# The chunked linear recurrence of a hybrid decoder layer under one list scheduler with the delta rule, with other planning weights

## The chip, the cores and the metric

The kernel runs on one core of a Trainium2 chip. The core has a matrix engine (TensorE, PE in the profile; its weight loads are shown as PEld), VectorE (DVE), ScalarE (ACT), GpSimd (POOL) and SyncE (SP), which issues transfers. Each takes its own instructions strictly in the order in which they were written, and waits at the head of its queue until semaphores of the others allow the next one. The metric is the device time of one execution in microseconds; the kernel before takes 1797.59 us, the median of three runs (1796.06 to 1799.65).

## The reference

One decoder layer on 512 tokens of width 1024, all float32: a SwiGLU block, a mixer, a second SwiGLU block, each with an RMS norm ahead and a residual, and a last norm. The mixer projects the normed input once and cuts the columns into two branches:

```python
o_h = hgrn2_chunked(q_h, k_h, hi, log_f)          # 8 heads: S = diag(f) S + k^T v, o = S^T q
o_h = rmsnorm(o_h, hgrn_out_norm) * silu(hg)
...
qkv = silu(causal_short_conv(concat([gq, gk, gv]), conv_w))
o_g = gated_delta_chunked(q_g, k_g, cv, beta, g)  # 16 value heads: S = a (I - beta k k^T) S + beta k v^T
o_g = rmsnorm(o_g, gdn_out_norm) * silu(gz)
...
y = sigmoid(gate_h) * (o_h @ w_branch_hgrn) + sigmoid(gate_g) * (o_g @ w_branch_gdn)
return y @ w_out
```

The first recurrence has a decay for each channel, so its scores inside a chunk are built by halves (blocks of 1, 2, 4 up to 64 positions). The delta rule needs the inverse of a unit lower triangular matrix of each chunk and head.

## The kernel before, in words

Every product with a weight is made in three float32r passes: a weight slab of 128x512 is loaded (`raw`, three buffers), split into a rounded part on ScalarE (`whi`) and the rest on VectorE (`wlo`, five buffers), and `mm3` adds three matmuls for each block of 128. A product of a transposed projection has 24 matmuls of 512 columns, one of an untransposed pair (`wn`, names V, G and z) 96 of 256 columns. The time axis of 512 is cut into four chunks of 128.

The program has four stretches: the first SwiGLU block, the first recurrence, the delta rule, and the merge with the output projection and the second SwiGLU block.

*The first recurrence.* `ORDER` (L33) is an order written out by hand: Q, F, V and G are projections of a head or a pair of heads, S the scores of two heads (`h_scores`, L513), O a head's output (`h_out`, L563), D the decays of the delta rule (`decays`). What is emitted so is interleaved by the framework's own scheduler, with priorities. In `h_scores` each of seven levels has products `pl` on PE (L538, L548), masked copies on VectorE (L541) or copies on ScalarE (L552), and updates of `qp` (VectorE, L556) and `ke` (GpSimd, L557). `h_out` carries the state over the chunks (L575 to L585) and norms the output with a power on GpSimd (L594).

*The delta rule* is planned by `Desk`, a list scheduler in the kernel. Each piece of work is a generator that asks for an engine and a duration, a buffer, an event or a lag. `Desk.run` steps through a planned time, gives the engine to the ready request of lowest rank, and lets the generator emit its instructions, in an order that the framework then leaves as it is. Only planned durations stand behind that order; the chip runs the queues as they were written. `product` (rank 9, the lowest) takes the dense products in the order in which `loader` chose them from `DENSE`; sixteen gate products (t) are taken when none of the list is allowed. The planned weights:

```python
LAG = 2.8                                     # every transfer
yield "use", "POOL", .62 + .0016 * n * w      # one step of the solve, two instructions
yield "use", "POOL", 1.2; yield "lag", .3     # a power on GpSimd, then its reader on VectorE
```

For each of eight pairs of value heads: `g_e` loads a row of decays to all partitions (gb, L653) and makes exponentials; `g_n` norms the key with a power on GpSimd (L695), whose reader is L700 on VectorE, and makes the score products (pgq, L712) and the matrix (n2, L727); `g_b` sends its diagonal blocks through DRAM (L745, L752), solves them on GpSimd in 31 steps of two instructions (L764, L765), and sends the result back through DRAM (L769 and L776, both on SP); `g_inv` copies it (L800), transposes it (L807) and completes the inverse with products (L821, L831); `g_rec` runs the recurrence over the chunks (L883 to L922), norms with another power (L935) and transposes the output (pto, L952). `keep` writes it to DRAM (od).

The buffers of the first recurrence are reused by the delta rule: `room` claims them, and `more` claims those of the branch outputs once product y7 is done. Both recurrences draw on gb, of which there are two buffers: heads hold qp in it, and `g_e` loads into it.

Of the kernel before, what the change touches and what calls it, by code (L numbers as in the profile page):

```python
# [8 lines left out]
F32 = mybir.dt.float32  # L9
# [23 lines left out]
ORDER = (  # L33
    "Q1 Q0 F5 F0 F1 V0 G0 S0 Q2 O0 Q3 O1 F2 F3 V1 G1 D0 S1 Q4 O2 Q5 O3 F4 V2 G2 S2 Q6 O4 Q7 O5 F6 F7 V3 "
    "G3 S3 O6 O7 "
)
# [7 lines left out]
WB = 5  # L44
# [4 lines left out]
LAG = 2.8  # L49
# [290 lines left out]
def mixer(tc, mp, e):  # L340
# [40 lines left out]
    def natural(i, use):  # L381

        sl = [slab(wn[i][:, q * 512:(q + 1) * 512]) for q in range(4)]
        for half in range(2):
            pt = psd.tile([P, T], F32, tag="mm", name="pnat")
            for s in range(2):
                part(sl, pt, 2 * half + s)
                with tc.high_priority():
                    use(2 * half + s, pt[:, s * 256:(s + 1) * 256])

    def part(sl, pt, t):
        for k in range(KD):
            hi, lo = sl[k // 2]
            c = slice((k % 2) * 256, (k % 2) * 256 + 256)
            mm3(pt[:, t % 2 * 256:t % 2 * 256 + 256], uh[:, k, t * P:(t + 1) * P], ul[:, k, t * P:(t + 1) * P],
                hi[:, c], lo[:, c], k == 0, k == KD - 1)

    def gate(t, o, g):

        th = places["thg"]("thg", (P, 256))  # L400
        act.activation(th, o, AF.Tanh, scale=rhalf[:, t:t + 1])
        dve.scalar_tensor_tensor(g[:, t], th, 1.0, o, op0=ALU.add, op1=ALU.mult)

    def normed(src, out):
        pt = dense(src, KD, ux)
        with tc.high_priority():
            dve.tensor_tensor(out, pt, rbc, op=ALU.mult)

# [27 lines left out]
    def decays():  # L436
        pab = dense(wab, KD, ux, m=64)
        dt_b, a_log = dta[:, 0:1], dta[:, 1:2]
        ab = h[:64, 0]
        pool.memset(ab, 0.0)  # L440
        z = h[:64, 1]
        dve.tensor_tensor(z, pab[:64], rbc[:64], op=ALU.mult)
        z2 = h[:16, 2]
        dve.tensor_scalar(z2, z[:16], dt_b, None, op0=ALU.add)
        w = [h[:16, 3 + i] for i in range(4)]

        dve.scalar_tensor_tensor(w[0], z2, -1.0, z2, op0=ALU.mult, op1=ALU.min)
        act.activation(w[0], w[0], AF.Exp)
        dve.tensor_scalar(w[1], w[0], 1.0, None, op0=ALU.add)
        act.activation(w[2], w[1], AF.Ln)  # L450
        dve.scalar_tensor_tensor(w[3], w[1], 1.0, w[0], op0=ALU.subtract, op1=ALU.subtract)
        dve.tensor_tensor(w[2], w[2], w[3], op=ALU.subtract)
        dve.scalar_tensor_tensor(w[2], z2, 0.0, w[2], op0=ALU.max, op1=ALU.add)
        ea = tm("ea", (16, 1))
        act.activation(ea, a_log, AF.Exp)
        dve.tensor_scalar(ab[:16], w[2], ea, -1.0, op0=ALU.mult, op1=ALU.mult)
        act.activation(ab[32:48], z[32:48], AF.Tanh, scale=0.5)
        dve.tensor_scalar(ab[32:48], ab[32:48], 1.0, 0.5, op0=ALU.add, op1=ALU.mult)
        pn = ps("pn")
        for c in range(NT):  # L460
            pe.transpose(pn[:, c * 64:(c + 1) * 64], ab[:, c * P:(c + 1) * P], ident[:64, :64])
        act.copy(nat, v3(pn[:, :256], NT))
        pg = ps("pg")
        pe.matmul(pg[:, 0:64], tri, g_nat, start=True, stop=True)
        pe.matmul(pg[:, 64:128], ones, g_nat, start=True, stop=True)
        dve.tensor_copy(gx[:, 0:2], pg[:, :128].rearrange("p (a b c) -> p a b c", a=2, b=NT))
        dve.tensor_tensor(ek, gend, gam, op=ALU.subtract)
        act.activation(eg, gam, AF.Exp)
        act.activation(eend, gend, AF.Exp)
        act.activation(ek, ek, AF.Exp)  # L470
# [3 lines left out]
        gt = h[:16, 7]  # L474
        dve.tensor_copy(gt, pgt[:16])
        sp.dma_start(gtd, gt)

    def together(*gens):
        gens = list(gens)
        while gens:  # L480
            gens = [g for g in gens if next(g, gens) is not gens]


    def h_q(hd_):
        qs = ta("qs")
        normed(wt[hd_], qs)
        th = ta("th")
        act.activation(th, qs, AF.Tanh, scale=0.5)
        qq = places[("fs", "ut")[hd_ % 2]]("qq", (P, NT, 192))
        dve.scalar_tensor_tensor(qq[:, :, :P], v3(th, NT), 1.0, v3(qs, NT), op0=ALU.add, op1=ALU.mult)  # L490
        return qq

    def h_f(hd_):
        fs = ta("fs")
        normed(wt[8 + hd_], fs)
        act.activation(fs, fs, AF.Tanh, scale=0.5)
        f = places["at"]("f")
        dve.tensor_scalar(f, fs, cf[:, 1, hd_:hd_ + 1], cf[:, 0, hd_:hd_ + 1], op0=ALU.mult, op1=ALU.add)
        ke = places[("kn", "vb")[hd_ % 2]]("ke")
        dve.tensor_scalar(ke, fs, cf[:, 2, hd_:hd_ + 1], cf[:, 1, hd_:hd_ + 1], op0=ALU.mult, op1=ALU.add)  # L500
        return f, ke

    def h_v(p_):
        v = places["n2"]("v", (P, NT, 256))
        natural(p_, lambda t, o: act.activation(v[:, t], o, AF.Copy, scale=rcol[:, t:t + 1]))
        return v

    def h_g(p_):
        g = places["gz"]("hg", (P, NT, 256))
        natural(4 + p_, lambda t, o: gate(t, o, g))  # L510
        return g

    def h_scores(hd_, qq, f, ke, res):  # L513
        qp = places["gb"]("qp")
        dve.tensor_tensor(v3(qp, NT), qq[:, :, :P], v3(f, NT), op=ALU.mult)
        q4 = qp.rearrange("p (c g b) -> p c g b", c=NT, b=2)
        dve.tensor_copy(qq[:, :, P:192], q4[:, :, :, 1])
        at = places["on"]("ah", (P, NT, P))
        fl = f
        ln_ = "ab"[hd_ % 2]  # L520
# [4 lines left out]
        for i in range(2):  # L525
            dve.tensor_tensor(at[:, 2 * i:2 * i + 2], v3(pd[i][:, :384], 2)[:, :, :P], mid(ident, 2), op=ALU.mult)
        for li, hh in enumerate((1, 2, 4, 8, 16, 32, 64)):
            n2 = T // (2 * hh)
            av = at.rearrange("p c (g two b) -> p c g two b", two=2, b=hh)
            if hh == 1:  # L530
                for i in range(2):
                    dve.copy_predicated(av[:, 2 * i:2 * i + 2, :, 1, 0], mid(hm[:, li].bitcast(I32), 2),
                                        v3(pd[i][:, :384], 2)[:, :, P:192])
            elif hh <= 16:
                pl = ps("pl", ln_)
                qv = qp.rearrange("p (c g two b) -> p c g two b", c=NT, two=2, b=hh)
                for c in range(NT):
                    pe.matmul(pl[:, c * 64:(c + 1) * 64], ke[:, c * P:(c + 1) * P], qv[:, c, :, 1],  # L538
                              start=True, stop=True)
                for c in range(NT):  # L540
                    dve.copy_predicated(av[:, c, :, 1], v3(hm[:, li].bitcast(I32), 64 // hh),  # L541
                                        v3(pl[:, c * 64:(c + 1) * 64], 64 // hh))
            else:
                pl = ps("pl", ln_)
                for c in range(NT):
                    for b in range(64 // hh):
                        s0 = 2 * b * hh
                        pe.matmul(pl[s0:s0 + hh, c * hh:(c + 1) * hh], ke[:, c * P + s0:c * P + s0 + hh],  # L548
                                  qp[:, c * P + s0 + hh:c * P + s0 + 2 * hh], start=True, stop=True)
                for b in range(64 // hh):  # L550
                    s0 = 2 * b * hh
                    act.copy(at[s0:s0 + hh, :, s0 + hh:s0 + 2 * hh], v3(pl[s0:s0 + hh, :NT * hh], NT))  # L552
# [4 lines left out]
            pool.tensor_tensor(kv[:, :, 0], kv[:, :, 0], bc(fv[:, :, 1], hh), op=ALU.mult)  # L557
            fn = (places[("x", "we")[hd_ % 2]] if hh == 1 else places[("w", "ft")[hd_ % 2]] if hh == 2 else tm)(f"fl{hh}", (P, n2))
            dve.tensor_tensor(fn, fv[:, :, 0], fv[:, :, 1], op=ALU.mult)
            fl = fn  # L560
            yield
        res += [qp, ke, at, fl]

    def h_out(hd_, qp, ke, at, fe, v, g):
        hs = slice((hd_ % 2) * P, (hd_ % 2) * P + P)
# [3 lines left out]
        kn = places[("gm", "qm")[hd_ % 2]]("hkn", (P, NT - 1, P))  # L569
# [736 lines left out]
```

## Time and profile before

| | |
|---|---|
| median of three runs | 1797.59 us |
| the profiled execution | 1803.54 us, its span 1801.8 us |
| PE busy | 1698.8 us (94%), 9362 matmuls |
| VectorE, ScalarE, GpSimd busy | 953.7, 698.5, 303.7 us |
| mean granted clock of PE | 0.967 |

The page cuts the span into 40 slices of 45 us:

```profile
PE   7999999999999989799798889889999999999997
...
DVE  4544443346586557447576667645454444444333
...
POOL 2000000001121122630532552620000100000001
PEclk9999999999999969899899999899999999999998
```

A digit is the busy share in tenths, and the last line the clock that the throttle granted to PE, in tenths of full speed. Slices 14 to 28 hold the delta rule. Matmuls are pipelined and their ends are modelled, so "busy" on PE says that work was there, not that it ran at its peak; at half clock the same work takes twice as long and counts as busy throughout.

### The profile page before, as it was taken

What the parts mean: (1) busy time and instruction counts of PE and PEld (TensorE: products, weight loads), DVE (VectorE), ACT (ScalarE), POOL (GpSimd) and SP (SyncE); (2) the same over time, 40 slices, a digit from 0 to 9 for tenths busy, and PEclk for the clock granted to TensorE, in tenths of its full rate; (3) what the DMA queues carried; (4) which work ended last, traced back from release to release, by engine and by line L of the source; (5) the groups of instructions that cost most, each with busy time, mean ns of one, the idle gap of its engine ahead of it and who ended that gap; (6) DMA issues with size and microseconds to landing.
All of it is one profiled execution on the core that took longest, in us unless ns stands there. A gap on an engine that the chain in (4) does not pass through costs nothing. (4 is left out here: it accounts for less than half of the span.)

```text
span 1801.8 us, 25958 instructions
## 1 busy us (share of the span) xinstructions
PE 1698.8 (94%) x9362; PEld 1441.1 (80%) x9362; DVE 953.7 (53%) x1992; ACT 698.5 (39%) x1525; POOL 303.7 (17%) x629
## 2 busy tenths in 40 slices
PE   7999999999999989799798889889999999999997
PEld 5888888889989977578686778678788888888887
DVE  4544443346586557447576667645454444444333
ACT  4433333332343325255455455334433433333222
POOL 2000000001121122630532552620000100000001
PEclk9999999999999969899899999899999999999998
DMA  4223333432222114334134233335753333333333
GB/s 150 93 95 100 94 96 114 114 103 71 71 66 71 42 50 134 102 91 115 47 97 117 62 95 96 96 84 169 232 161 109 123 94 100 94 100 92 96 97 112
DMA packets 142561, 182.16 MB, mean 101 GB/s; under 512 B 53072, under 2 KB 59728, under 8 KB 142432
## 3 DMA queue, kind: packets, MB, share of 16 engines
q1 hardware_dynamic: 142432, 180.49, 34.1%
q8 instruction: 74, 1.21, 0.3%
q14 instruction: 55, 0.45, 0.1%
HBM read 163.64 MB, written 16.81 MB: 100 GB/s over the span
## 5 line engine op out<-in xcount | busy, mean ns | idle before, releaser
L176 PE MATMUL pmm<-uh,whi 128*128 128x512 f32 x1288 | 522.8, 406 | 17.0 <-ACT whi L171 6.0
L178 PE MATMUL pmm<-uh,wlo 128*128 128x512 f32 x1288 | 509.8, 396 | 5.3 <-DVE wlo L1120 5.3
L177 PE MATMUL pmm<-ul,whi 128*128 128x512 f32 x1288 | 510.6, 397 | 2.6 <-DVE ul L203 2.4
L171 ACT CAST whi<-raw 128x512 fp32r<-128x512 f32 (+1 forms) x391 | 239.4, 612 | 542.9 <-PE pmm L177 485.0
L172 DVE TENSOR_TENSOR wlo<-raw,whi 128x512 fp32r<-128x512 f32 (+1 forms) x391 | 269.4, 690 | 296.2 <-ACT whi L171 295.6
L176 PEld LDWEIGHTS pmm<-uh,whi 128*128 128x128 f32 x1288 | 246.4, 191 | 68.8 <-ACT whi L171 6.0
L178 PEld LDWEIGHTS pmm<-uh,wlo 128*128 128x128 f32 x1288 | 245.6, 191 | 58.7 <-DVE wlo L1120 5.9
L177 PEld LDWEIGHTS pmm<-ul,whi 128*128 128x128 f32 x1288 | 246.2, 191 | 54.6 <-DVE ul L203 6.4
L176 PE MATMUL pnat<-whi,uh 128*128 128x256 f32 x512 | 153.3, 301 | 0.6 <-DVE ci L627 0.6
L178 PE MATMUL pnat<-whi,ul 128*128 128x256 f32 x512 | 146.1, 286 | 0.0
L177 PE MATMUL pnat<-wlo,uh 128*128 128x256 f32 x512 | 145.8, 285 | 0.0
L176 PE MATMUL pmm<-gh,whi 128*128 128x512 f32 (+1 forms) x374 | 141.0, 377 | 0.0
L178 PE MATMUL pmm<-gh,wlo 128*128 128x512 f32 (+1 forms) x374 | 140.9, 377 | 0.0
L177 PE MATMUL pmm<-gl,whi 128*128 128x512 f32 (+1 forms) x374 | 140.8, 377 | 0.0
L1120 DVE TENSOR_TENSOR wlo<-raw,whi 128x512 fp32r<-128x512 f32 x144 | 99.4, 694 | 76.6 <-ACT whi L1118 75.4
L1118 ACT CAST whi<-raw 128x512 fp32r<-128x512 f32 x144 | 88.8, 619 | 129.1 <-PE pmm L177 77.7
L214 POOL TENSOR_TENSOR acc<-acc,sqt 128x512 f32<-128x512 f32 x24 | 32.8, 1366 | 583.6 <-ACT sqt L212 583.2
L764 POOL TENSOR_TENSOR fm<-gfs,ft 128x60 f32<-128x60 f32 (+24 forms) x248 | 88.6, 357 | 169.7 <-DMA ft<-hmask 138.0
L176 PEld LDWEIGHTS pnat<-whi,uh 128*128 128x128 f32 x512 | 98.6, 193 | 2.1 <-DVE ci L627 0.8
L177 PEld LDWEIGHTS pnat<-wlo,uh 128*128 128x128 f32 x512 | 98.7, 193 | 0.8
L178 PEld LDWEIGHTS pnat<-whi,ul 128*128 128x128 f32 x512 | 98.4, 192 | 0.1
L765 POOL TENSOR_TENSOR ft<-ft,fm 128x60 f32<-128x60 f32 (+24 forms) x248 | 92.6, 373 | 19.4
(345 smaller groups left out, 2228.3 us busy)
## 6 DMA issues: line engine op xcount, KB each, us to landing
raw<-wt SPq DMA_DIRECT2D x128, 256.0 KB
raw<-w1a SPq DMA_DIRECT2D x88, 256.0 KB
raw<-w1b SPq DMA_DIRECT2D x88, 256.0 KB
raw<-wn SPq DMA_DIRECT2D x64, 256.0 KB
raw<-w2b SPq DMA_DIRECT2D x45, 256.0 KB
raw<-w2a SPq DMA_DIRECT2D x40, 256.0 KB
raw<-wbg SPq DMA_DIRECT2D x32, 256.0 KB
gb<-gtd SPq DMA_DIRECT2D x16, 256.0 KB
```

The lines of the kernel that those rows point to most:

```text
L171: act.copy(hi[:, :f], raw[:, :f])
L172: dve.tensor_tensor(lo[:, :f], raw[:, :f], hi[:, :f].bitcast(F32), op=ALU.subtract)
L176: pe.matmul(pt, ah, bh, start=first, stop=False)
L177: pe.matmul(pt, ah, bl, start=False, stop=False)
L178: pe.matmul(pt, al, bh, start=False, stop=last)
L214: pool.tensor_tensor(acc, acc, s, op=ALU.add)
L764: pool.tensor_tensor(tv, bc(m[:, j + 1:, j], w), t[:, j:j + 1, :w].to_broadcast([P, n, w]), op=ALU.mult)
L765: pool.tensor_tensor(t[:, j + 1:, :w], t[:, j + 1:, :w], tv, op=ALU.add)
L1118: act.copy(hi, raw)
L1120: dve.tensor_tensor(lo, raw, hi.bitcast(F32), op=ALU.subtract)
```

## The change

`ORDER`, the functions that emitted the first recurrence by hand and `room` are removed. Its projections go ahead of the list that `Desk` draws on, and each piece becomes a generator with ranks, buffers and planned durations as the delta rule has them. The arithmetic is the same.

```diff
 DENSE = (
+    "F0 Q0 F1 Q1 V0 G0 F2 Q2 F3 Q3 V1 G1 D0 F4 Q4 F5 Q5 V2 G2 F6 Q6 F7 Q7 V3 G3 "
     "k0 q0 k1 q1 y0 y1 y2 y3 v0 v1 y4 y5 y6 y7 z0 k2 q2 v2 v3 z1 ...
-LAG = 2.8
+LAG = dict(raw=3.2, gb=4, nb=5, m=6, nt=4, tq=8, out=4)
+EASE = 2.5
```

The scores and the output of a head are one generator. Its `ke` updates run in a thread of their own:

```diff
+    def h_head(i):
+        yield "on", ("Q", i), ("F", i)
...
+        yield "get", "gb", 1
...
+        def keys(li, kv, fv, hh):
+            yield "use", "POOL", .88
+            pool.tensor_tensor(kv[:, :, 0], kv[:, :, 0], bc(fv[:, :, 1], hh), op=ALU.mult)
+            D.fire(("ke", i, li))
...
+                yield "get", ln_, 1
+                yield T_(.92 if hh <= 16 else .5)
...
+            D.start((2, i), keys(li, kv, fv, hh))
+            yield V(270)
             dve.tensor_tensor(qv[:, :, 1], qv[:, :, 1], bc(fv[:, :, 0], hh), op=ALU.mult)
```

In the delta rule the powers get slack on both sides, a solve step its new weight, and the store of the solve goes from SyncE to GpSimd:

```diff
         dve.tensor_scalar(rk, sm[:, 0, 0:4], 4.0 * EPS, None, op0=ALU.add)
+        yield "lag", EASE
         yield "use", "POOL", 1.2
         pool.tensor_tensor(rk, rk, mhalf[:, :4], op=ALU.pow)
-        yield "lag", .3
+        yield "lag", EASE
...
-            yield "use", "POOL", .62 + .0016 * n * w
+            yield "use", "POOL", .7 + .004 * n * w
...
-        yield "lag", .3
-        yield S
-        sp.dma_start(nt.rearrange("b q i c -> (b q) i c"), t)
-        yield "lag", LAG
+        yield "use", "POOL", .6
+        pool.dma_start(nt.rearrange("b q i c -> (b q) i c"), t)
+        yield "lag", LAG["nt"]
```

The buffers that pass from one recurrence to the other are claimed one by one, as the heads give them back, and a product is chosen when the events that it needs have come:

```diff
+    def claim(name, tag, n, shape, zero=False):
+        G.setdefault(name, [])
+        yield "on", ("free", tag)
+        for j in range(n):
+            yield "get", "w_" if tag == "w" else tag, 1
+            G[name].append(pl(tag, shape))
...
     def choose():
...
+            need = {"Q": [("pd", i - 2)] if i > 1 else [], "F": [("L", i - 4)] if i > 3 else [],
+                    "V": [("pair", i - 2)] if i > 1 else [], "G": [("pair", i - 2)] if i > 1 else [], "D": [],
+                    "y": [("O", 5), ("S", 6), ("S", 7)], ...
+            if all(n in D.at for n in need) and not (k in "qkv" and under >= CONVS):
+                todo.remove(x)
+                return x
         return gates.pop(0) if gates else None
```

`product` now also makes V, G and D, and waits for each branch input (`("O", kt)`) within a y product. The state buffers (s) of both recurrences are counted too. Neither SwiGLU block nor the merge is touched.

More of the change, by code (lines that the diff above doesn't have):

```diff
@@ L379, in mixer @@
     eye4 = e["hmask"][:, 5:9].rearrange("p a (i c) -> p (a i) c", c=8)
[L381 to L407, printed above, removed]
     dve.tensor_scalar(rhalf, rcol, 0.5, None, op0=ALU.mult)
@@ L434, in mixer @@
     gtd = dr.tile([16, T], F32, name="gtd")
-    def decays():
-        pab = dense(wab, KD, ux, m=64)
+    md = dr.tile([KD, P, T], F32, name="md")
+    td = dr.tile([2 * KD, P, T], F32, name="td")
+    od = dr.tile([VH, P, T], F32, name="od")
+    D = Desk(mm=2, a=2, b=2, d=1, e=1, ta=TA, tm=6, thg=1, raw=RB, w=WB, tq=1, n2=2, gz=2, fs=1, ut=1, kn=3, gm=1,
+             qm=2, gb=2, ln=1, at=4, vb=4, t64=2, on=2, ft=1, x=1, we=1, w_=1, s=3)
+    V = lambda n: ("use", "DVE", 0.21 + 0.001 * n)
+    A = lambda n: ("use", "ACT", 0.2 + 0.0009 * n)
@@ L438, in decays, with place @@
+    T_ = lambda n: ("use", "PE", n)
+    S = ("use", "SP", 0.4)
+    taken = {}
+    def place(tag, name, shape, n):
+        taken[tag] = taken.get(tag, 0) + 1
+        if taken[tag] == n:
+            D.fire(("free", tag))
+        return places[tag](name, shape)
+    def decays(pab):
         dt_b, a_log = dta[:, 0:1], dta[:, 1:2]
         ab = h[:64, 0]
+        yield "use", "POOL", .6
         pool.memset(ab, 0.0)
         z = h[:64, 1]
+        yield "on", "rbc"
+        yield *V(512), 1
@@ L474, in decays, with h_q @@
         gt = h[:16, 7]
+        yield V(512)
         dve.tensor_copy(gt, pgt[:16])
+        D.put("d")
+        yield S
         sp.dma_start(gtd, gt)
[L478 to L484, printed above, removed]
+        yield "lag", LAG["out"]
+        D.fire("decays")
+    def h_q(i, pt):
+        yield "get", "ta", 2
+        yield "on", "rbc"
+        yield *V(512), 1
         qs = ta("qs")
-        normed(wt[hd_], qs)
+        dve.tensor_tensor(qs, pt, rbc, op=ALU.mult)
+        D.put("mm")
+        yield A(512)
@@ L487, in h_q, with h_f @@
         th = ta("th")
         act.activation(th, qs, AF.Tanh, scale=0.5)
-        qq = places[("fs", "ut")[hd_ % 2]]("qq", (P, NT, 192))
+        tag = ("fs", "ut")[i % 2]
+        yield "get", tag, 1
+        yield V(512)
+        qq = hq[i] = place(tag, "qq", (P, NT, 192), 4)
         dve.scalar_tensor_tensor(qq[:, :, :P], v3(th, NT), 1.0, v3(qs, NT), op0=ALU.add, op1=ALU.mult)
-        return qq
-    def h_f(hd_):
+        D.put("ta", 2)
+        D.fire(("Q", i))
+    def h_f(i, pt):
+        yield "get", "ta", 1
+        yield "on", "rbc"
+        yield *V(512), 1
@@ L494, in h_f @@
         fs = ta("fs")
-        normed(wt[8 + hd_], fs)
+        dve.tensor_tensor(fs, pt, rbc, op=ALU.mult)
+        D.put("mm")
+        yield A(512)
         act.activation(fs, fs, AF.Tanh, scale=0.5)
[L497 to L514, printed above, removed]
+        yield "get", "at", 1
+        yield V(512)
+        f = place("at", "f", (P, T), 8)
+        dve.tensor_scalar(f, fs, cf[:, 1, i:i + 1], cf[:, 0, i:i + 1], op0=ALU.mult, op1=ALU.add)
@@ new lines, in h_f, with h_v @@
+        tag = ("kn", "vb")[i % 2]
+        yield "get", tag, 1
+        yield V(512)
+        ke = place(tag, "ke", (P, T), 4)
+        dve.tensor_scalar(ke, fs, cf[:, 2, i:i + 1], cf[:, 1, i:i + 1], op0=ALU.mult, op1=ALU.add)
+        hf[i] = f, ke
+        D.put("ta")
+        D.fire(("F", i))
+    def h_v(i, t, o):
+        yield A(300)
+        act.activation(hv_[i][:, t], o, AF.Copy, scale=rcol[:, t:t + 1])
+        if t % 2:
+            D.put("mm")
+        if t == 3:
+            D.fire(("V", i))
@@ L524, in h_scores @@
                       start=True, stop=True)
-        for i in range(2):
-            dve.tensor_tensor(at[:, 2 * i:2 * i + 2], v3(pd[i][:, :384], 2)[:, :, :P], mid(ident, 2), op=ALU.mult)
+        D.put(tag_q)
+        D.fire(("pd", i))
+        yield "get", "on", 1
+        at = place("on", "ah", (P, NT, P), 8)
+        for q in range(2):
+            yield V(256)
+            dve.tensor_tensor(at[:, 2 * q:2 * q + 2], v3(pd[q][:, :384], 2)[:, :, :P], mid(ident, 2), op=ALU.mult)
+        def keys(li, kv, fv, hh):
+            yield "use", "POOL", .88
+            pool.tensor_tensor(kv[:, :, 0], kv[:, :, 0], bc(fv[:, :, 1], hh), op=ALU.mult)
+            D.fire(("ke", i, li))
+        fl, held = f, "at"
         for li, hh in enumerate((1, 2, 4, 8, 16, 32, 64)):
@@ L546, in h_scores @@
                     for b in range(64 // hh):
                         s0 = 2 * b * hh
[L548 to L552, printed above, removed]
+                        yield A(4 * hh)
@@ L568, in h_out @@
             pe.transpose(pk[:, c * P:(c + 1) * P], ke[:, c * P:(c + 1) * P], ident)
-        kn = places[("gm", "qm")[hd_ % 2]]("hkn", (P, NT - 1, P))
+        tag_n = ("gm", "qm")[i % 2]
+        yield "get", tag_n, 1
+        yield A(384)
+        kn = place(tag_n, "hkn", (P, NT - 1, P), 4)
         act.copy(kn, v3(pk[:, :(NT - 1) * P], NT - 1))
+        D.put("d")
+        yield "get", "a", 1
         po = ps("po", "a")
@@ L585, in h_out @@
                     dve.scalar_tensor_tensor(s2, s, fe[:, c:c + 1], pu[:, :P], op0=ALU.mult, op1=ALU.add)
+                    D.put("s")
                 s = s2
-        ss = tm("hss", (P, NT))
-        on = places[("ln", "t64")[hd_ % 2]]("hon", (P, NT, P))
+                D.put("b")
+        D.put("s")
+        D.put(tag_n)
+        D.put(tag_k)
+        D.put("gb")
+        D.put("on")
+        D.put(held)
+        tag_o = ("ln", "t64")[i % 2]
+        yield "get", tag_o, 1
+        yield "get", "tm", 2
+        ss, rho = tm("hss", (P, NT)), tm("hrho", (P, NT))
+        on = place(tag_o, "hon", (P, NT, P), 4)
         for c in range(NT):
+            yield A(300)
             act.activation(on[:, c], po[:, c * P:(c + 1) * P], AF.Square, accum_out=ss[:, c:c + 1])
-        rho = tm("hrho", (P, NT))
+        yield V(4)
         dve.tensor_scalar(rho, ss, 4.0 / P, 4.0 * EPS * 4.0 * P, op0=ALU.mult, op1=ALU.add)
+        yield "lag", EASE
+        yield "use", "POOL", 1.2
         pool.tensor_tensor(rho, rho, mhalf[:, :NT], op=ALU.pow)
+        yield "lag", EASE
+        yield V(4)
         dve.tensor_tensor(rho, rho, rcol, op=ALU.mult)
         for c in range(NT):
+            yield V(150)
             dve.scalar_tensor_tensor(on[:, c], po[:, c * P:(c + 1) * P], rho[:, c:c + 1], g[:, c, hs],
                                      op0=ALU.mult, op1=ALU.mult)
+        D.put("a")
+        D.put("tm", 2)
+        D.fire(("o", i))
+        yield "get", "d", 1
+        yield T_(.46)
         pt = ps("pt")
@@ L602, in h_out, with h_pair @@
         gn = cs[:, C_HN:C_HN + 1]
-        o2 = op[hd_]("oh", (P, 2, T), F32R)
-        oh, ol = o2[:, 0], o2[:, 1]
+        o2 = op[i]("oh", (P, 2, T), F32R)
+        oh, ol = o_h[i] = o2[:, 0], o2[:, 1]
+        yield A(560)
         act.activation(oh, pt, AF.Copy, scale=gn)
+        yield V(560)
         dve.scalar_tensor_tensor(ol, pt, gn, oh.bitcast(F32), op0=ALU.mult, op1=ALU.subtract)
-        return oh, ol
-    md = dr.tile([KD, P, T], F32, name="md")
-    td = dr.tile([2 * KD, P, T], F32, name="td")
-    od = dr.tile([VH, P, T], F32, name="od")
-    D = Desk(mm=2, a=2, b=2, d=1, e=1, ta=TA, thg=1, gb=2, raw=RB, w=WB, on=2, tq=1)
-    V = lambda n: ("use", "DVE", 0.21 + 0.001 * n)
-    A = lambda n: ("use", "ACT", 0.2 + 0.0009 * n)
-    T_ = lambda n: ("use", "PE", n)
-    S = ("use", "SP", 0.4)
+        D.put("d")
+        D.put(tag_o)
+        D.fire(("O", i))
+    def h_pair(p_):
+        yield "on", ("o", 2 * p_), ("o", 2 * p_ + 1)
+        D.put("n2")
+        D.put("gz")
+        D.fire(("pair", p_))
     def conv(k, i, pt, out, n):
@@ L962, in keep @@
         sp.dma_start(to, tile_)
-        yield "lag", LAG
+        yield "lag", LAG["out"]
         D.put(tag)
@@ L1044, in more @@
         G["tp"].append(e_[:, 3].rearrange("p (a b) -> p a b", a=8))
-    def step(k, i):
-        if k in "QFVG":
-            hp[k, i] = {"Q": h_q, "F": h_f, "V": h_v, "G": h_g}[k](i)
-        elif k == "S":
-            hr[2 * i], hr[2 * i + 1] = [], []
-            together(*[h_scores(j, hp["Q", j], *hp["F", j], hr[j]) for j in (2 * i, 2 * i + 1)])
-        elif k == "O":
-            o_h[i] = h_out(i, *hr[i], hp["V", i // 2], hp["G", i // 2])
-        elif k == "D":
-            decays()
-    for w in ORDER.split():
-        step(w[0], int(w[1:]))
+        D.fire("more")
@@ L1112, in maker @@
     def maker(key, raw):
-        yield "lag", LAG
+        yield "lag", LAG["raw"]
         yield "get", "w", 1
@@ L1126, in product @@
     def product():
-        total = len(todo) + len(gates) + len(line)
-        for n in range(total):
+        for n in range(len(todo) + len(gates) + len(line)):
             yield "on", ("line", n + 1)
             x = k, i = line[n]
-            if k == "z":
+            if k in "VGz":
+                if k != "z":
+                    yield "get", {"V": "n2", "G": "gz"}[k], 1
+                    to = place(*{"V": ("n2", "v"), "G": ("gz", "hg")}[k], (P, NT, 256), 4)
+                    (hv_ if k == "V" else hg_)[i] = to
+                else:
+                    to = G["gz"][i % 3]
                 for t in range(4):
@@ L1148, in product @@
                     if t % 2:
-                        D.start((1, n), zgate(i, t - 1, pt[:, :256]))
-                        D.start((1, n), zgate(i, t, pt[:, 256:]))
+                        for r in (t - 1, t):
+                            o = pt[:, r % 2 * 256:r % 2 * 256 + 256]
+                            D.start((1, n), h_v(i, r, o) if k == "V" else gate(x, to, r, o))
                 continue
             yield "get", "mm", 1
-            for q in range(2):
+            m = 64 if k == "D" else P
@@ L1172, in product, with norm @@
             D.start((5, n), th)
             if x == ("y", 7):
-                more()
-                D.fire("more")
+                D.fire("branch")
         D.fire("projected")
-    room()
+    def norm():
+        yield "lag", 9.0
+        D.fire("rbc")
+    G["tp"] = [places["tp"]("gtp", (P, 8, 32))]
+    D.start((0,), norm())
     D.start((3, -1), loader())
     D.start((9,), product())
+    for i in range(8):
+        D.start((2, i), h_head(i))
+    for i in range(4):
+        D.start((2, i), h_pair(i))
@@ new lines, in mixer @@
+    for name, tag, n, shape in (("kn", "kn", 3, tb), ("qm", "qm", 2, tb), ("n2", "n2", 2, big),
+                                ("gz", "gz", 2, (P, NT, 256)), ("at", "at", 4, tb), ("vb", "vb", 4, tb),
+                                ("m", "fs", 1, (P, 32, 32)), ("tq", "ln", 1, (P, 32, 8)), ("x", "x", 1, col),
+                                ("we", "we", 1, col), ("w", "w", 1, col)):
+        D.start((6, 0), claim(name, tag, n, shape))
+    D.start((6, 0), claim("ut", "ut", 1, (P, 8, P), True))
@@ L1181, in mixer @@
+    D.start((6, 0), claim("t64", "t64", 2, (64, 8, 64), True))
+    D.start((6, 0), second())
+    D.start((6, 0), more())
     for u in range(8):
```

282 lines of the change are left out of this document (171 added, 111 removed).

## The prediction

> **What bounds the kernel now.** I read first the page's slices, then busy time by stretch, then the waits of PE, DVE and SP, then the timeline around the longest of them. PE is busy for 94% of the span, and the low slices all lie between 642 and 1287 us. By stretch (columns: stretch, length, busy us of PE, PEld, DVE, ACT, POOL with counts, granted clock, DMA share, GB/s):
>
> ```profile
> 380.40:642.00 261.60, 259.45 (x1833) 235.26 (x1831) 161.50 (x451) 90.48 (x205) 44.40 (x54) 1.00 0.22 64
> ...
> 642.00:668.00 26.00, 19.97 (x127) 17.61 (x126) 12.39 (x53) 4.55 (x19) 9.45 (x13) 0.61 0.12 40
> 668.00:1287.00 619.00, 550.03 (x3523) 468.60 (x3523) 379.77 (x878) 291.85 (x793) 208.66 (x524) 0.94 0.37 105
> ```
>
> The first recurrence (to 642) has PE idle for 2.1 of 261.6 us: nothing is to be won there, only lost. The delta rule (668 to 1287) has it idle for 69.0 us, and in the 26 us between them PE runs 127 matmuls at a clock of 0.61, with 6.0 us idle. The clock costs more: the sum over the eleven stretches between 644 and 1201 us in which it was granted at half is
>
> ```profile
> 644.30:661.40 17.10, 15.84 (x104) 14.48 (x104) 8.29 (x36) 2.23 (x7) 6.36 (x9) 0.50 0.00 1
> ...
> sum 95.40, PE 65.13 PEld 55.38 DVE 54.45 ACT 29.18 POOL 19.34; mean PE 5.92 PEld 5.03 DVE 4.95 ACT 2.65 POOL 1.76
> ```
>
> PE worked 65.13 us at half speed, which is 32.6 us lost. So PE lost 69.0 + 6.0 + 32.6 = 107.6 us between 642 and 1287. PE is the bound even so: the last pair's output transposes (pto, L952) end at 1263.2, and the gate products after them keep PE full to 1287.
>
> Why it idles stands in the queues of the others. SyncE, its issues and its longest waits:
>
> ```profile
> 614.31 2.26 SPq L1108 DMA_DIRECT2D raw<-wt  x3
> 662.78 0.33 SPq L653 DMA_DIRECT2D gb<-gtd  x1
> ```
> ```profile
> SPq L769 <- POOL ft L765: 81.4, 7, 18.6
> ...
> SPq L653 <- PE po L577: 46.2, 1, 46.2
> ```
>
> For 46.2 us SP issues nothing: the first gb load (L653) stands at its head and waits for a buffer that a recurrence head still holds. No weight comes in, so after 642 PE has only the last heads' small matmuls. VectorE's waits in the delta rule, and one of them close up (VectorE, then GpSimd):
>
> ```profile
> DVE sm L700 <- POOL sm L695: 36.9, 5, 11.0
> DVE gtp L800 <- DMA ggz<-nt: 17.1, 1, 17.1
> DVE gtp L800 <- DMA x<-nt: 12.9, 3, 10.0
> DVE x L800 <- DMA x<-nt: 11.8, 3, 7.5
> ```
> ```profile
> 941.62 0.69 DVE L789 TENSOR_TENSOR gvb<-ptv,sm 128x512 f32<-128x512 f32 x1 [0.36 <-PE ptv L787]
> 952.27 0.17 DVE L700 SCALAR_TENSOR_TENSOR sm<-nat,sm 128x8 f32<-128x8 f32 x1 [9.95 <-POOL sm L695]
> ```
> ```profile
> 951.06 0.20 POOL L765 TENSOR_TENSOR ft<-ft,fm 128x8 f32<-128x8 f32 x1
> 951.22 1.02 POOL L695 TENSOR_TENSOR sm<-sm,mhalf 128x4 f32<-128x4 f32 x1
> ```
>
> GpSimd's power (L695) stands behind the 62 steps of the previous pair's solve. The planner put L700 on VectorE as if the solve were shorter, so VectorE stands still for 9.95 us with slabs and state updates queued behind it. L800 is the same with the way from the solve through DRAM. Together 78.7 us, and PE's waits are those of the instructions queued behind:
>
> ```profile
> PE pw L896 <- DVE x L887: 14.9, 2, 9.3
> PE pq L821 <- DVE gut L807: 14.9, 3, 12.8
> PE pw L896 <- DVE gx L887: 10.0, 2, 5.9
> PE pgq L712 <- DVE gqm L718: 7.6, 1, 7.6
> PE pgq L712 <- DVE x L789: 7.5, 1, 7.5
> ```
>
> **The change, part by part.** It takes away no arithmetic; all of it is order.
>
> *Weights of solve steps.* The old weight sums over 31 steps to 31 x 0.62 + 0.0016 x 1560 = 21.7 us, the new one to 31 x 0.7 + 0.004 x 1560 = 27.9 us. The eight solves in the trace take 25.7 to 29.5 us (first L764 to last L765: 715.0 to 744.5, 924.6 to 951.3 and so on). So what hangs on a solve was planned some 6 us early for each pair, and no longer is.
>
> *Transfers and slack around powers.* The new lags are 4 to 8 us for the ways through DRAM, with 2.5 us on either side of a power. In the built order I counted PE's work between a pair's second score product (L712) and its first inverse product (L821), at the start-to-start distances of the trace (0.2275 us for 512 columns, 0.12 for 256, 0.215 for each pass of a 256-column float32 product, and so on). Before, the pairs have 50, 62, 53, 66, 56, 56, 67 and 59 us there; after, 64, 75, 71, 74, 73, 69, 76 and 73. What it takes when nothing is in the way: pair 2, from the end of L712 at 832.2 to the end of the transposes at 894.0, 61.8 us. Five of eight lay below that, none does now. By this the 69.0 us of idle PE and their half clock (the 65.13 us less some 18 in the 26 us stretch, so 23.5 us lost) go. I keep 3 us for pair 0, whose margin is 2.5 us, and 1.5 us for each of six other places where the new order is just met (9 us).
>
> *The first recurrence in the list.* The gb buffers are now counted for both users, so no load stands 46 us at SP's head, and in the built order the last heads' steps lie between the products k0 to z0. The 26.0 us hold 19.97 - 9.1 = 10.9 us of work at full clock (18.2 us ran at half); 15.1 us go. What it may cost: 56 level steps and 24 state steps are placed by hand-given weights. These match their rows: L538's four products 0.90 us for 0.92, L556 0.485 for 0.48, L541 0.242 for 0.27, L557 0.771 to 0.880 for 0.88. The lower bound is 0, the upper 80 times the longest wait of such a step in the last stretch (0.72 us), 58 us. I take 5, near the 2.1 us of now.
>
> *The store of the solve, from SP to GpSimd.* SP loses a wait (81.4 us in seven) behind which weight loads queued; GpSimd's queue has the next pair's power and solve behind the issue. No row shows a transfer issued by GpSimd. SP's store is followed by its dependent load after 1.7 us at best (884.39 to 886.07) and 3.7 at worst (745.46 to 749.20). A gain is possible only through SP, and that is in the sum already; the loss is 0 to 5 us for a pair, 3 taken. Pairs 1 to 7 have 7 us or more of margin and hide it; without that cover it would cost 3 us each, 21 in all. For pair 0 it is in the 3 us kept.
>
> *The end.* The gates t0 to t4 are now used up earlier, and the last pair's transposes come after t15 and 14 merge products. From the last L912 to L952 it took 11.4 us (1248.7 to 1260.1); 6 + 14 products cover 4.6. Of the 6.8 left, 4.4 are there today (wait at 1287.07 for uh), so 2.4 more, and 1.6 for the last two loads of od. I keep 4. The store and reload of od lie under some 56 merge products (12.7 us).
>
> *Clock.* I keep 10 us of the 32.6, four or five pieces like those of 6.8 us with 4 to 6 us of PE work in each. The Trainium skill, page "TensorE: Matmul & The Clock Gate", section "HAM oscillation — how this bites in real kernels", ties a re-throttle to PE gaps over about 3.4 us; by that the kept waits would cost no clock and the sum be 1711. The trace disagrees in one place: 17.1 us at half from 644.3 on, with no gap over 0.72 us around it. The sum goes by the trace.
>
> Sum: 107.6 lost, kept 9 + 3 + 5 + 4 + 10 = 31, so 76.6 us less. The profiled execution took 1803.5 us (span 1801.8), which gives 1726.9; it lay 5.9 us above the median of the runs, 1797.6, so against that **1721 us**.
>
> **Rivals.** (A) *Half stays.* VectorE is still in order, and a power still comes right behind a solve (the built GpSimd order has the powers of pairs 2, 3, 4 and 6 there); if half the waits only move, 34.5 us of idle and 11.8 of clock stay in place of the 22 kept: 1745. For it: 36.9 us in only five waits. Against: margins above 61.8 everywhere. (B) *The chain of the last pair becomes the bound.* Its L712 to L952 has 119.6 us of PE work beside it after; before it took 1121.5 to 1263.2, 141.7 us. If it takes that again, 22 us of idle and 5 of clock: 1748. The slack around its two powers, up to 10 us by the weights against the 1.1 to 1.6 us of a power, lengthens it too. Against: in the 141.7 the solve waited for pair 6's until 1143.6, some 8 us. (C) *Slower: the recurrence under the list.* VectorE serves slabs ahead of level steps; if two slab subtractions (L1120, 0.69 us each) stand ahead of each of the 80 steps when PE wants it, that is 80 x 1.4 = 112 us against 76.6 won: 1833. It decides from 0.96 us a step. For it: the region is full now, so each wait counts in full. Against: PE's spacing between a head's levels is about 4 us in the built order, while a level needs about 2.8 (0.9 on PE, 4 x 0.242 + 0.485 on VectorE, hand-overs). (D) *No effect:* the waits are the transfers' own, 1797.
>
> **How the numbers follow.** Forecast 0.67, A 0.15, B 0.08, C 0.08, D 0.02. The forecast's own range is 1700 to 1750 (kept terms from 10 to 60 us). 1696 to 1780 leaves out C, D and the tails, about 0.16. A difference under 0.2% (3.6 us) can't be told from none. Faster: forecast, A and B, 0.90; same 0.02; slower 0.08.
>
> **What would show it.** Right: L653's successor no longer tens of us at SP's head; VectorE's waits for the power and for the reload of the solve under 25 us together; PE's idle time in the mixer near 25 us; half clock under 35 us. Wrong: new PE waits on pl, po or pks in the first recurrence, t gates used up long before the last pto, or a GpSimd transfer that lands after 5 us or more.

## The result, and the profile after

The changed kernel takes 1703.68 us, the median of four runs (1703.18 to 1704.43), beside 1796.82 us for the kernel before on the same chip: a ratio of 0.9479, with a 95% interval of 0.9463 to 0.9496. The forecast was 1721 us, with a range from 1696 to 1780.

The profiled execution has a span of 1702.6 us. First its page, the slices of PE and of its clock:

```profile
PE   7999999999999999999999999999999999999997
...
PEclk9999999999999999999999999999999999999998
```

The low slices in the middle are gone, in the busy time and in the clock. Busy time by stretch (columns as in the prediction); the last gate product ends at 1187, where it was 1287:

```profile
380.40:642.00 261.60, 258.67 (x1866) 234.77 (x1865) 168.65 (x478) 94.79 (x219) 50.81 (x62) 1.00 0.24 70
642.00:668.00 26.00, 26.00 (x164) 21.91 (x164) 18.77 (x50) 14.71 (x42) 5.37 (x7) 1.00 0.31 91
668.00:1187.00 519.00, 510.65 (x3436) 440.04 (x3435) 364.05 (x841) 275.78 (x751) 225.43 (x528) 0.99 0.42 118
```

From 668 us to the last gate product PE is idle for 8.4 us, where it was 69.0. The stretch from 642 to 668 is full. The first recurrence pays 2.9 us of idle time against 2.1. At half clock there are two stretches left between 642 and 1187 us (columns as above):

```profile
684.60:688.00 3.40, 3.40 (x19) 3.40 (x18) 2.16 (x4) 1.65 (x7) 0.00 (x0) 0.50 0.37 124
988.40:991.80 3.40, 3.38 (x10) 2.59 (x9) 3.40 (x9) 1.67 (x3) 2.91 (x7) 0.50 0.59 166
```

So 6.8 us of work at half speed, 3.4 us lost, where it was 65.13 and 32.6. VectorE's waits between 668 and 1187 have one line for the power; none is left for the reload of the solve (waiting engine, tile, line, releaser: us in all, times, longest):

```profile
DVE sm L808 <- POOL sm L803: 4.2, 3, 1.9
```

The power of pair 3, on VectorE and then on GpSimd (L803 and L808 are the L695 and L700 of before, L877 is the store of the solve). The power shown of before was pair 4's, for which VectorE waited 9.95 us; for pair 3's it waited 11.0:

```profile
837.47 0.69 DVE L746 SCALAR_TENSOR_TENSOR x<-th,cy 128x512 f32<-128x512 f32 x1 [0.48 <-ACT th L743]
839.62 0.17 DVE L808 SCALAR_TENSOR_TENSOR sm<-nat,sm 128x8 f32<-128x8 f32 x1 [1.46 <-POOL sm L803]
```
```profile
837.39 0.20 POOL L874 TENSOR_TENSOR ft<-ft,fm 128x8 f32<-128x8 f32 x1
837.89 0.63 POOL L877 DMA_DIRECT2D nt<-ft  x1 [0.30 <-POOL ft L874]
838.55 1.03 POOL L803 TENSOR_TENSOR sm<-sm,mhalf 128x4 f32<-128x4 f32 x1
```

The power still stands behind the previous pair's solve. What is new is the place of its reader: VectorE gets to pair 3's 1.46 us too early, where it was 11.0, and to pair 4's 0.93, where it was 9.95. SyncE's waits for the two transfers in question (L886 reloads the solve, L759 is the gb load):

```profile
SPq L886 <- DMA nt<-ft: 22.0, 5, 11.5
...
SPq L759 <- PE po L660: 1.2, 1, 1.2
```

The gb load is held for 1.2 us, where it was 46.2. At the solve SyncE still stands for 22.0 us, now at the reload; before, it stood for 81.4 us at the store and 6.0 at the reload.

### The profile page after: what moved, and what is told of

It reads as the page before. It is cut to its first block, busy times and chain, and to the rows that moved or that the text cites. A ratio compares the mean times of both kernels' runs of the same rounds, so it can differ in the third digit from the quotient of the medians.

```text
span 1702.6 us, 25965 instructions
## 1 busy us (share of the span) xinstructions
PE 1666.9 (98%) x9362; PEld 1418.3 (83%) x9362; DVE 954.9 (56%) x1992; ACT 699.8 (41%) x1525; POOL 324.0 (19%) x637
## 5 line engine op out<-in xcount | busy, mean ns | idle before, releaser
L174 PE MATMUL pmm<-uh,whi 128*128 128x512 f32 (+1 forms) x1288 | 522.3, 406 | 15.1 <-ACT whi L169 5.6
L175 PE MATMUL pmm<-ul,whi 128*128 128x512 f32 (+1 forms) x1288 | 505.8, 393 | 2.6 <-DVE ul L201 2.4
L176 PE MATMUL pmm<-uh,wlo 128*128 128x512 f32 (+1 forms) x1288 | 505.4, 393 | 0.0
L169 ACT CAST whi<-raw 128x512 fp32r<-128x512 f32 x326 | 198.9, 611 | 447.8 <-PE pmm L175 411.3
L170 DVE TENSOR_TENSOR wlo<-raw,whi 128x512 fp32r<-128x512 f32 x326 | 223.8, 688 | 259.5 <-ACT whi L169 259.2
L174 PEld LDWEIGHTS pmm<-uh,whi 128*128 128x128 f32 (+1 forms) x1288 | 243.7, 189 | 65.0 <-ACT whi L169 5.6
L175 PEld LDWEIGHTS pmm<-ul,whi 128*128 128x128 f32 (+1 forms) x1288 | 243.4, 189 | 52.4 <-DVE ul L201 6.4
L176 PEld LDWEIGHTS pmm<-uh,wlo 128*128 128x128 f32 (+1 forms) x1288 | 242.9, 189 | 52.8 <-DVE wlo L170 0.3
L1226 ACT CAST whi<-raw 128x512 fp32r<-128x512 f32 x209 | 129.3, 620 | 208.2 <-PE pmm L175 122.7
L1228 DVE TENSOR_TENSOR wlo<-raw,whi 128x512 fp32r<-128x512 f32 x209 | 147.4, 708 | 118.0 <-ACT whi L1226 114.5
L873 POOL TENSOR_TENSOR fm<-gfs,ft 128x60 f32<-128x60 f32 (+24 forms) x248 | 95.6, 385 | 95.4 <-DMA ft<-hmask 63.7
L874 POOL TENSOR_TENSOR ft<-ft,fm 128x60 f32<-128x60 f32 (+24 forms) x248 | 100.8, 406 | 19.4
```

Of the source, the lines that this page charges most:

```text
L169: act.copy(hi[:, :f], raw[:, :f])
L170: dve.tensor_tensor(lo[:, :f], raw[:, :f], hi[:, :f].bitcast(F32), op=ALU.subtract)
L174: pe.matmul(pt, ah, bh, start=first, stop=False)
L175: pe.matmul(pt, ah, bl, start=False, stop=False)
L176: pe.matmul(pt, al, bh, start=False, stop=last)
L873: pool.tensor_tensor(tv, bc(m[:, j + 1:, j], w), t[:, j:j + 1, :w].to_broadcast([P, n, w]), op=ALU.mult)
```

## The experiments

The theory: what PE lost in the delta rule came from VectorE standing behind powers and reloads that the planner had put too early, so the weights won it, and the joining of the recurrences won only the stretch from 642 to 668. The main rival: the joining won it, since pairs start earlier and the list of products is longer. Ratios are against the kernel before on the same chip, with 95% intervals.

**e1_weights, the weights alone.** In the kernel before, with its order written out by hand:

```diff
-LAG = 2.8
+LAG = dict(raw=3.2, gb=4, nb=5, m=6, nt=4, tq=8, out=4)
+EASE = 2.5
...
-            yield "use", "POOL", .62 + .0016 * n * w
+            yield "use", "POOL", .7 + .004 * n * w
```

with each lag taken from its entry, and EASE around the two powers.

> The kernel before with the new planning weights alone (solve step, transfer lags, slack around powers); the first recurrence keeps its order written by hand, the store of the solve stays on SyncE. Theory (the weights made the gain in the delta rule, 69.0 us of idle PE and 23.5 us of half clock there, the joining only the 15.1 us of the stretch 642 to 668): about 1720 us (1708 to 1735), and the first gb load still stands some 46 us at SP's head. Rival (the joining made it, by the longer list of products and the earlier start of the pairs): 1775 us or more.

1727.67 us (1722.78 to 1730.28), ratio 0.9599 (0.9570 to 0.9628): 69.8 us less than before. SyncE still stands at the first gb load (it is L654 here), with nothing issued from 615.3 to 660.4 us, and the stretch behind it is much as it was (19.97 us and 0.61 before). VectorE's waits for the power, 36.9 us before, are down to 5.8 in two, and none is left for the reload of the solve:

```profile
613.07 2.25 SPq L1111 DMA_DIRECT2D raw<-wt  x3
660.41 0.33 SPq L654 DMA_DIRECT2D gb<-gtd  x1
```
```profile
642.00:668.00 26.00, 18.21 (x121) 15.63 (x122) 11.77 (x50) 6.58 (x23) 8.21 (x11) 0.68 0.17 47
```
```profile
DVE sm L702 <- POOL sm L697: 5.8, 2, 4.8
```

**e2_joined, the joining alone.** In the changed kernel, the weights of before:

```diff
-LAG = dict(raw=3.2, gb=4, nb=5, m=6, nt=4, tq=8, out=4)
-EASE = 2.5
+LAG = dict(raw=2.8, gb=2.8, nb=2.8, m=2.8, nt=2.8, tq=2.8, out=2.8)
+EASE = .15
...
-            yield "use", "POOL", .7 + .004 * n * w
+            yield "use", "POOL", .62 + .0016 * n * w
```

> The changed kernel with the old weights (solve step 0.62 + 0.0016 n w, every lag 2.8, 0.3 us in all around a power); the first recurrence is in the list, the store of the solve on GpSimd. Theory (weights): about 1782 us (1768 to 1795), with VectorE waiting over 50 us for powers and for the reload of the solve. Rival (joining): about 1715 us (1704 to 1730).

1774.26 us (1772.13 to 1774.59), ratio 0.9859 (0.9835 to 0.9882): 23.2 us less than before. 642 to 668 is full at full clock, and in the delta rule VectorE waits as before:

```profile
DVE sm L808 <- POOL sm L803: 32.6, 6, 7.5
DVE x L910 <- DMA gln<-nt: 18.6, 3, 11.0
DVE gtp L910 <- DMA gln<-nt: 9.7, 2, 9.5
```

60.9 us together, where the theory had asked for over 50. The two parts add up, 69.8 + 23.2 = 93.0 us, and the whole change gave 93.1 (that they meet so closely is chance, as the runs of e1_weights spread over 7.5 us). The main rival falls; the joining is worth more than the theory had said (23 against 15).

**e4_solve, e5_ease, e6_lag: one weight of before at a time** in the changed kernel: the solve step, then EASE at .15, then every lag at 2.8.

> The changed kernel with the old weight of a solve step alone; lags and slack stay new. Theory (a solve planned 6 us short puts the powers' readers too early on VectorE; the slack of 2.5 us on both sides takes up some 3 of the 6): 1715 to 1735 us, with VectorE waiting 15 to 30 us for the power. Rival (the lags and the slack alone are enough): 1704 us, within 4 us.

> The changed kernel with the slack around the powers cut from 2.5 us to 0.15 us on each side; solve weight and lags stay new. Theory (a power takes 1.0 to 1.7 us and is planned at 1.2, and the solve ahead of it is planned at its length, so the slack covers only what the solve and the hand-overs miss, a few us at a pair): 1706 to 1716 us. Rival (the slack is what keeps VectorE from standing behind the powers): 1725 us or more, with over 20 us of VectorE waiting for the power.

> The changed kernel with every lag of a transfer back at 2.8 us; solve weight and slack stay new. Theory (the way of the solve through DRAM takes some 9 us from its end to the transposes, planned at 6 instead of 12.6): 1725 to 1740 us, with VectorE waiting over 20 us at the copy of the reload. Rival (the margin of 64 to 76 us comes from the solve's weight alone): 1704 us, within 5 us.

| weight of before put back | median (lowest to highest) | ratio, interval | VectorE's wait for the power | for the reload |
|---|---|---|---|---|
| solve step | 1729.04 (1727.84 to 1731.67) | 0.9612, 0.9588 to 0.9636 | 17.8 us, 4 times | none |
| slack around powers | 1707.88 (1707.50 to 1709.96) | 0.9506, 0.9484 to 0.9529 | 7.0 us, 2 times | 0.6 us |
| lags | 1732.17 (1726.85 to 1735.66) | 0.9635, 0.9608 to 0.9662 | 16.0 us, 5 times | 12.2 us, 7 times |

Against 1703.68 us that is 25.4, 4.2 and 28.5 us, all three times within what the theory had asked for. The changed kernel itself took 1705.80 us in a second set of runs (e9_after), so 4.2 may be as little as 2.1. The three together, in e2_joined, cost 70.6 us, more than their sum of 58.1. The expectation of e6_lag was missed in one point: over 20 us of waiting were expected at the copy of the reload, and 12.2 are there, with 16.0 more at the power. So the lags are at work on both waits; that a shorter lag plans the whole chain of a pair early, and its powers with it, is the likely reading. Its lines:

```profile
DVE sm L808 <- POOL sm L803: 16.0, 5, 5.4
DVE x L910 <- DMA gln<-nt: 8.0, 4, 2.9
DVE gtp L910 <- DMA gln<-nt: 4.2, 3, 2.6
```

In e4_solve a solve is planned at 21.7 us, 6.2 below the new weight, and 17.8 us of waiting remain after the slack has taken its share.

**e8_over, the same error with the other sign.** In the changed kernel a solve step is planned 0.2 us longer:

```diff
-            yield "use", "POOL", .7 + .004 * n * w
+            yield "use", "POOL", .9 + .004 * n * w
```

> The changed kernel with a solve step planned 0.2 us too long (0.9 in place of 0.7), 6.2 us for a solve: the same error as the old weight's, with the other sign. Theory (what is planned late costs only where the last chain ends the mixer, what is planned early stops a whole in-order queue): 1703 to 1710 us, VectorE waiting under 5 us for the power. Rival (the error costs the same either way, since the chain of the pairs is as long as the product list): 1720 to 1730 us.

1702.34 us (1701.27 to 1705.61), ratio 0.9465 (0.9442 to 0.9489): no slower than the changed kernel beside it (e9_after, 1705.80, 1702.92 to 1706.22), if anything 3 us faster. So 6.2 us below the new weight costs 25 us, and 6.2 us above it nothing that can be measured. The two are not quite the same error, though: the solves of the changed kernel's trace take 25.6 to 33.3 us, five of eight more than the 27.9 of the new weight, and the 34.1 us planned here cover the longest. Measured against the trace, e4_solve plans every solve of its own (26.1 to 31.6 us) 4 to 10 us short, while the 34.1 us of e8_over lie 1 to 8 us above those of the changed kernel. No wait for the power of the key norm is left on VectorE; what comes in its place stands at the end, where the last pair's chain runs without products between its steps (PE's waits, 1187 to 1205 us, where the changed kernel has one wait of 3.9 us):

```profile
PE pks L993 <- DVE s L1033: 2.8, 2, 1.4
PE pog L1020 <- DVE x L1011: 1.3, 1, 1.3
PE pw L1006 <- DVE x L997: 0.4, 1, 0.4
```

**e7_gb, the gb wait alone.** In the kernel of e1_weights, two gb buffers of its own for the first four loads:

```diff
-            gb = places["gb"]("gb", (P, NT, P))
+            gb = places["ge" if hd_ < 4 else "gb"]("gb", (P, NT, P))
```

> The kernel before with the new weights, as in the run of the weights alone (1727.67 us), and with two gb buffers of its own for the first four gb loads, which thereby don't wait for a head. Theory (the 45 us in which SyncE stands at the first gb load are what the joining took away): 1710 to 1716 us, with no wait of over 10 us for gb. Rival (the last heads' chain itself holds PE in that stretch, whatever SyncE does, and only the joint list fills it): 1722 us or more.

1720.22 us (1719.10 to 1720.39), ratio 0.9570 (0.9551 to 0.9588). That is 7.5 us less than e1_weights with the ranges apart, but on another chip; by the ratios it is 5.2 us, and their intervals overlap a little. The time lies between what theory and rival had asked for. SyncE no longer stops, and 642 to 668 is nearly full, but the stretch behind it isn't, and the wait that costs PE most from 642 us on is the recurrence's own:

```profile
642.00:668.00 26.00, 25.16 (x174) 21.76 (x172) 23.19 (x73) 15.44 (x42) 8.76 (x11) 1.00 0.25 86
668.00:700.00 32.00, 22.99 (x106) 17.59 (x107) 13.96 (x41) 7.93 (x28) 5.50 (x7) 0.79 0.07 24
```
```profile
PE pt L602 <- DVE hon L598: 6.6, 2, 3.3
PE pmm L177 <- DVE ggz L997: 5.5, 2, 3.9
```

The last two heads' output norms hold PE at 674 and 685 us, for 3.3 us each, with half clock after both; the same line stands in e1_weights, 6.6 us in two. So SyncE's wait explains some 5 to 7.5 us of the 24.0 by which the changed kernel lies below e1_weights. Where the rest lies can be counted in the traces, as PE's idle time and half of its work at half clock from 642 us to the last gate product: 29.6 us in e7_gb, 11.8 in the changed kernel. Of the 17.8 us between them, 11.8 lie ahead of 700 us (15.3 against 3.5), where the last heads run without products beside them. The other 6 come later, above all at two waits for VectorE (ggz at 758 us, 3.95 us, and x at 1090 us, 3.1 us), and no run isolates them. That the last heads get products only because both recurrences stand in one list is argued from these traces; no run changes it alone.

**e3_store_sp and e10_store_sp, the store of the solve back on SyncE.** In the changed kernel:

```diff
-            yield "use", "POOL", .6
-            pool.dma_start(nt.rearrange("b q i c -> (b q) i c"), t)
+            yield "lag", .3
+            yield S
+            sp.dma_start(nt.rearrange("b q i c -> (b q) i c"), t)
```

> The changed kernel with the store of the solve back on SyncE (planned as a lag of 0.3 and an issue of 0.4 us), nothing else. Theory (the margin between score products and inverse hides the way of the store, on either queue): 1704 us, within 4 us. Rival (SyncE stands at the store and weight loads queue behind it, as in the kernel before, 81.4 us in seven): 1712 to 1725 us, with PE waiting on whi or wlo. A second rival (the transfer by GpSimd lands later, up to 8 us after its issue in the profile, and costs time): 1695 to 1700 us.

> The store of the solve back on SyncE once more, beside the changed kernel itself: theory (the queue of the store makes no difference that counts): within 3 us of the changed kernel; rival (it is faster by what half an issue and the later landing cost at each pair): 1697 to 1701 us, 3 us or more below the changed kernel.

> The changed kernel as it is, for comparison with the run of the store on SyncE on the same chip: 1703.7 us.

e3_store_sp took 1701.03 us (1699.15 to 1703.29), ratio 0.9457 (0.9429 to 0.9486), and e10_store_sp 1701.21 us (1697.42 to 1703.23), 0.9455 (0.9433 to 0.9478), beside 1705.80 us for the changed kernel itself (e9_after, 0.9478, 0.9455 to 0.9502). Both medians are lower, by 2.7 and 4.6 us. The intervals of the ratios overlap, but they share the scatter of the kernel before; run against run on one chip, five of the six of e10_store_sp lie below the lowest of e9_after. So the store on SyncE is faster by a few us, and the theory of e10_store_sp (within 3 us) was missed in favour of its rival (3 us or more below; its upper bound of 1701 us was just missed). The cause is not isolated: in the traces PE's wait for uh (the head outputs, reloaded from DRAM, that the merge products read) after the gate products is 2.1 and 2.2 us with the store on SyncE and 3.9 in both with it on GpSimd, which would be some 1.8 us of it. The second rival's premise does not hold: a store from GpSimd landed after 4.7 us at most, and where the reload came 9 us after the store (719.89 to 729.08), it had landed after 2.4 us and SyncE was issuing other loads. The rival, that weight loads would queue behind the store, falls: with the new weights SyncE waits 16.6 us at it in four, where it was 81.4 in seven. The two runs and e8_over are the fastest seen, and moving the store to GpSimd had no part in the gain.

## Why the prediction was right

*The bound and its cause.* 107.6 us were said to be lost between 642 and 1287 us: VectorE standing behind the power and the reload, SyncE behind gb, and half clock after each. The end of the gate products moved by 100 us in the traces; the span moved by 99 and the median time by 93, since the profiled execution of before lay 5.9 us above its median. The runs that put weights back one by one show VectorE's two waits coming back, and e1_weights, without the joining, still has the one for gb (45.0 us).

*The margins between score products and inverse.* They were said to be above what a pair needs everywhere. PE's waits between 642 and 1187 us have no line left for the transposes of the solve (14.9 us in three before), for pair 0 neither, whose margin was 2.5 us. One premise was too kind: what hangs on a solve "no longer is" planned early holds for three pairs only, as the other five solves now take 29.4 to 33.3 us against 27.9 planned. The slack and the margins took that up, all but the 4.2 us of waiting for the power.

*What was kept.* 31 us were kept for waits that remain, and 12.6 are there: 0.8 more in the first recurrence for 5, 8.4 in the delta rule for 9 + 3, nothing at the end for 4, and 3.4 of clock for 10. The difference of 18 us is the 17 us by which the forecast was high. The largest mis-sized term is the clock. With VectorE's long waits gone PE has gaps of at most 2.6 us there, and two of them were followed by half clock, a stretch of 3.4 us each. The Trainium skill ("TensorE: Matmul & The Clock Gate", section "HAM oscillation — how this bites in real kernels") ties a re-throttle to PE gaps over about 3.4 us; by that rule the kept waits would have cost no clock and the forecast been 1711, the nearer number. This trace doesn't bear it out to the letter either: the two stretches follow gaps of 1.79 and 2.59 us.

*The end.* The transposes came 11.3 us after the last pog end (1185.6 to 1196.9), against 11.4 taken from before. The last six gate products, the wait for uh (3.9 us; 4.4 before) and the 14 merge products, nearly all at half clock, filled that time, so nothing was left to wait for and the 4 us fell away.

*The step that was wrong in its reason.* "The gb buffers are now counted for both users, so no load stands 46 us at SP's head": the size of the stretch, 15.1 us, was laid to this alone. The joining gave 23.2, and e7_gb shows the gb wait to be worth 5 to 7.5 of it. By the traces the last heads' own chain is the larger part: the prediction saw that their steps would lie between products, but gave it no price of its own.

*The store.* 3 us were taken for a transfer issued by GpSimd. Its issue takes 0.6 us and it lands in 3.0 us (median); of this at most 4.6 us of the whole show in the time. The gain for SyncE was smaller than the 81.4 us it was to lose: it waits 22.0 us at the reload (15.8 in e9_after), where e3_store_sp has 16.6 at the store and 3.7 at the reload, so with the new weights the move freed a few us of SyncE at most.

*The rivals.* A (half the waits move) needed VectorE to stand elsewhere: 4.2 us are left. B (the last chain as the bound) shows only in e8_over, and the time is no longer there. C (the recurrence slower under the list) has a price of 0.8 us in all, far from 0.96 us a step.

## What to carry to other kernels

An order worked out ahead of time for in-order queues is only as good as its durations, and the errors are not alike: an instruction placed too early stops its whole queue and those that feed on it, and PE's clock after that, while one placed too late cost nothing in the one case tried, where other work filled the time. So plan waits on another engine's long work, and on ways through DRAM, at their traced length or above (here a solve planned 6.2 us below the new weight cost 25 us, and one planned 6.2 us above it, past the longest in the trace, nothing). And look for a queue that issues nothing for tens of microseconds: a transfer at its head that waits for a buffer holds every load behind it (46.2 us here, though freeing it alone was worth only 5 to 7.5).

## What the runs showed of the hardware

Half clock does not need a long gap, and the length of a gap doesn't decide alone. In the changed kernel it came after 1.79 us without a matmul (at 682 us), while gaps of 1.76 and 1.17 us went by without it. In the second trace of the same kernel (e9_after) the same gap of 1.79 us went by without it, and one of 1.99 us did not. In e5_ease one of 2.40 us went by. Over the twelve traces, from 380 to 1300 us, every gap of 2.59 us or more was followed by half clock (or fell into it), and between 1.8 and 2.4 us some were and some weren't. In the kernel before it also held for 17.1 us in which no gap passed 0.72 us and PE had 104 matmuls, 84 of them of 64 columns or fewer and the others of 128. Every stretch in these windows lasted 3.4 us or a whole multiple of it, up to those 17.1.

The transfer issued by GpSimd, in the view of its line (engine, operation, count: duration in ns, first and last start; then from issue to landing):

```profile
L877 POOL DMA_DIRECT2D nt<-ft x8: 588/631/759, 719.9 to 1121.1; - x8
...
DMA to landing us min/median/max: 2.0/3.0/4.7
```

From SyncE (the kernel before) the dependent load followed after 1.7 us in five of the six cases in which it waited for the store, and after 3.7 in the other, with an issue of 0.33 us.

The same 62 instructions of a solve took 25.7 to 29.5 us before and 25.6 to 33.3 us after, with GpSimd's busy time in the whole kernel up from 303.7 to 324.0 us. The four with VectorE busy for 79 to 87% of the time took 30.6 to 33.3 us, the two with 48 and 50% took 27.8 and 25.6; but one with 75% took 26.5, and what makes them slower wasn't tried.
